# Rounded w_out weights of the feed-forward layers: fetched by GpSimd's casting transfers in place of ScalarE's casts

## The chip, the cores and the metric

The kernel runs on one core of one Trainium2 chip. The metric is the device time of one execution in microseconds (us), the median of the runs. Besides the times there is one execution recorded by the hardware profiler, and its trace.

## The reference

One streaming-encoder block over 512 positions with 1024 features, all in float32, one layer deep, on one sequence:

```python
h = h + 0.5 * _swiglu(_rmsnorm(h, ffn1_norm[i]), ffn1_w_in[i], ffn1_w_out[i])
z = _rmsnorm(h, mix_norm[i]) @ w_in[i]
...
h = h + jnp.concatenate([y_conv, y_gla], axis=-1) @ w_out[i]
h = h + 0.5 * _swiglu(_rmsnorm(h, ffn2_norm[i]), ffn2_w_in[i], ffn2_w_out[i])
gate = jax.nn.sigmoid(_rmsnorm(h, ple_norm[i]) @ ple_w_gate[i])
h = h + gate * (p[i] @ ple_w_proj[i])
```

`_swiglu` multiplies by a first matrix (1024 x 5632: a gate and an up half), takes silu(gate) * up, 2816 features, and multiplies by a second matrix (2816 x 1024), named `ffn1_w_out` or `ffn2_w_out`. The mixer between the two feed-forward layers is a causal convolution beside a chunked gated linear attention; its output matrix is also called `w_out`, but the change does not touch it. Below, w_out is the second matrix of a feed-forward layer.

## The kernel before

**Two parts for each operand.** Every large product is done in float32r, a rounded float32. To keep float32 accuracy each operand is split in a high part, the value rounded to float32r, and a low part, the value minus the high part. A product is then three matmuls that add up in PSUM: high x high, high x low, low x high (`mm3`, L209). For a weight the high part is tile wh and the low part wl; for the activations of the second matrix they are actH and actL; the normalised input of the first matrix appears as hgH and hgL and sums of these.

**How a weight gets there.** `load` (L178) takes a plain float32 tile wr (`raw`, six buffers) and has SP's queue fill it from HBM. `parts` (L205) is `high` then `low`: `high` (L183) takes one of six wh and one of six wl buffers and casts wr into wh on ScalarE; `low` (L193) subtracts wh from wr on VectorE into wl. `added` (L198) is another way to a low part, used for weights of the next stage: ScalarE writes the rounded negative of wr into wl, and a transfer that GpSimd issues adds wr to it. A tile has up to 128 partitions x 1024 numbers, 512 KB.

**A feed-forward layer.** `ffn` (L608) goes over the 22 blocks of 128 hidden features in 11 pairs. Most pairs do the first matrix by Strassen's scheme, in seven units m1 to m7 of 24 matmuls over 256 columns each; in each layer a few pairs at the start are plain (units h0 to h7). The gate products of a pair give tile m, and `act_parts` (L658) splits it into actH (ScalarE) and actL (VectorE). The second matrix is taken in the cuts of L33, four hidden blocks each and a last one of six. `second` (L749) makes for each cut units that it calls pieces: one piece has a weight tile of 4 x 128 rows by 256 columns, and its run does 2 x 4 x 3 matmuls over 512 columns and adds the result to h. The last cut is in two halves of three blocks, so its pieces are 3 x 128 rows (384 KB) and 18 matmuls. Each cut has four pieces, the last one eight: 24 pieces a layer, 48 in all. In the text, piece (4,1) is the one of the last cut for columns 512 to 767 and its second half.

**The order.** The units of a layer stand in one list; pieces of a cut are spread between the units of the pairs that follow (two in each pair, after m2 and after m3), and at the end of the layer those of the last cut follow each other. `drive` (L588) goes over the list; each unit brings jobs with a lead, and a job with lead n is written n units ahead of its unit, those with the larger lead first. A piece has `get` (the plain load, lead 7) and `make` (`parts`, lead `AHEAD` = 4). Class `Ordered` (L36) fixes the order of TensorE's, VectorE's and ScalarE's instructions to the order in which the program writes them; so an instruction that waits holds everything behind it on its engine. For SP's and GpSimd's queues the order is left to the compiler, and so is which buffer of a tag a tile gets. Instructions of the ordered engines show L46 in the profile, the line of that class that calls the engine, whatever line they were written on.

**Work of the next stage.** Hooks at given units, such as ("m4", 10) and ("last", 4) of the first layer, load weights of the mixer and complete their low parts by GpSimd's adding transfers. In these stretches GpSimd has hardly anything else to do.

Of the kernel before, what the change touches and what calls it, by code (L numbers as in the profile page):

```python
# [9 lines left out]
F32R = mybir.dt.float32r  # L10
# [5 lines left out]
P = 128  # L16
# [46 lines left out]
def block_kernel(ctx: ExitStack, tc: tile.TileContext, a: dict, out: bass.AP):  # L63
    nc = tc.nc
    pe, dve, act, pool = (Ordered(tc, e) for e in (nc.tensor, nc.vector, nc.scalar, nc.gpsimd))
# [8 lines left out]
    wp = ctx.enter_context(tc.tile_pool(name="w", bufs=1))  # L74
# [5 lines left out]
    def nm(s):  # L80
        uid[0] += 1
        return f"{s}_{uid[0]}"
# [4 lines left out]
    def bt(dt=F32, s="a"):  # L87
        return big.tile([P, SEQ], dt, tag="A", bufs=NA, name=nm(s))
# [7 lines left out]
    def bank():  # L96
        return pp.tile([P, SEQ], F32, tag="mm", bufs=7, name=nm("ps"))
# [36 lines left out]
    def vec(name, c):  # L134
        return vcols[name, c]
# [42 lines left out]
    def load(src, k0, nk, c0, ncol):  # L178
        r3 = raw(nk, ncol)
        fetch(r3, src, k0, nk, c0, ncol)  # L180
        return r3

    def high(r3):  # L183

        nk, nc_ = r3.shape[1], r3.shape[2]
        hi = wp.tile([P, 1024], F32R, tag="wh", bufs=6, name=nm("wh"))
        lo = wp.tile([P, 1024], F32R, tag="wl", bufs=6, name=nm("wl"))
        h3 = hi[:, :nk * nc_].rearrange("p (k c) -> p k c", k=nk)
        l3 = lo[:, :nk * nc_].rearrange("p (k c) -> p k c", k=nk)
        act.copy(h3, r3)  # L190
        return h3, l3, r3

    def low(w, engine=dve):  # L193
        h3, l3, r3 = w
        engine.tensor_tensor(out=l3, in0=r3, in1=h3.bitcast(F32), op=ALU.subtract)
        return h3, l3
# [8 lines left out]
    def parts(r3):  # L205

        return low(high(r3))

    def mm3(ps, wh, wl, xh, xl, first, last):  # L209
        pe.matmul(ps, wh, xh, start=first, stop=False)  # L210
        pe.matmul(ps, wh, xl, start=False, stop=False)
        pe.matmul(ps, wl, xh, start=False, stop=last)
# [15 lines left out]
    def rows_of(w, k):  # L228

        part, kk = (w[k // 4], k % 4) if isinstance(w, list) else (w, k)  # L230
        return part[0][:, kk, :], part[1][:, kk, :]

    def zblock(w, x, mid={}):

        ps = bank()
        for k in range(DC):
            if k in mid:
                mid[k]()
            wh, wl = rows_of(w, k)
            mm3(ps, wh, wl, *x[k], k == 0, k == DC - 1)  # L240
        return ps
# [344 lines left out]
    AHEAD = 4  # L586
# [21 lines left out]
    def ffn(w_in, w_out, x, gname, given, first, rsb, hooks, plain):  # L608
# [4 lines left out]
        got = {}  # L613
# [135 lines left out]
        def second(cut):  # L749

            f0, f1 = cut
            last = f1 == CUTS[-1][1]
            kn = f1 - f0
            nk = kn // 2 if last else kn
            ps = {}

            def piece(n, g, begin, final, key=None):

                def get():
                    got[f0, n, g] = load(w_out, f0 + g * nk, nk, n * P, 2 * P)  # L760

                def make():
                    got[f0, n, g] = parts(got[f0, n, g])

                def run():
                    left = []
                    wh, wl = got.pop((f0, n, g))
                    for i in range(2):
                        if begin:
                            ps[n + i] = bank()  # L770
                        cs = slice(i * P, (i + 1) * P)
                        for kk in range(nk):
                            k = g * nk + kk
                            f = f0 + k
                            mm3(ps[n + i], wh[:, kk, cs], wl[:, kk, cs], *pairs[f // 2].acts[f % 2],
                                k == 0, k == kn - 1)
                        if final:
                            h = hT[n + i]
                            dve.scalar_tensor_tensor(out=h, in0=ps[n + i], scalar=0.5, in1=h,
                                                     op0=ALU.mult, op1=ALU.add)  # L780
                            if last:
                                hi = bt(F32R, "hgH")
                                act.activation(hi, h, AF.Copy, scale=vec(gname, n + i))
                                left.append((h, hi, vec(gname, n + i)))
                    if key:
                        hooks.get(key, lambda *_: None)()
                    if not left:
                        return []

                    def lower():  # L790
                        for h, hi, g in left:
                            lo = bt(F32R, "hgL")
                            dve.scalar_tensor_tensor(out=lo, in0=h, scalar=g, in1=hi.bitcast(F32),
                                                     op0=ALU.mult, op1=ALU.subtract)
                            nhg.append((hi, lo))

                    lower()
                    for h, *_ in left:
                        norm.add(h)

                return [(7, get), (AHEAD, make)], run

            if not last:
                return [piece(n, 0, True, True, ("g2", f0) if n == 0 else None) for n in range(0, DC, 2)]
            return ([piece(n, 0, True, False, ("last", n)) for n in range(0, 6, 2)],
                    [piece(n, 1, False, True, ("rest", n)) for n in range(0, 6, 2)]
                    + [piece(6, 0, True, False, ("rest", 6)), piece(6, 1, False, True, ("rest", 7))])

# [267 lines left out]
    k0 = zblock(wk[0], hg)  # L1076
# [312 lines left out]
    for k in range(4):  # L1389
        for n in range(3):  # L1390
            w, ps = half[n]
            wh, wl = rows_of(w, k)
# [303 lines left out]
    m1 = [kept(p_, "sq", bufs=3) for p_ in x_]  # L1696
    times(y_, a12, b21, first=True, last=True)
    b2 = [low(later_high(t)) if t is t2[1] else parts(t) for t in t2]
    pool.on, pool.last = True, None
    b3 = [added(later_high(t)) for t in t3]  # L1700
# [13 lines left out]
    body(0, 0, z0, *i0)  # L1714
    body(1, 0, z1, *i1)
    b1 = [parts(t1[0])]
    both = tmp("m", 2 * SEQ, bufs=1).rearrange("p (f c) -> p f c", f=2)
    for i in range(2):
# [76 lines left out]
```

## Time and profile before

| What | us |
|---|---|
| three runs | 947.73, 948.3, 947.78 |
| their median | 947.78 |
| the profiled execution, first to last instruction | 948.1 |
| first feed-forward layer, steady part of the span | 37 to 366 |
| mixer | 366 to 555 |
| second feed-forward layer | 555 to 886 |
| input embedding gate, final norm, output | 886 to 948 |

The bounds of the stages are read from the timeline and rounded to whole microseconds. The profile gives for each engine the busy time, the number of instructions, and the granted TensorE clock. A group of instructions is named by engine, operation and its output and inputs; "128x1024" is partitions by elements. Matmul ends are modelled, so two neighbours may seem to overlap; the distance of their starts is the safer number. The engines are PE (TensorE), PEld (its weight loads), DVE (VectorE), ACT (ScalarE), POOL (GpSimd) and SP (SyncE, which only issues transfers here).

### The profile page before, as it was taken

How to read it: one execution, taken by the hardware profiler on the slowest of the kernel's cores; microseconds unless marked ns; L12 is line 12 of the kernel's file. 1: busy time of each engine (PE TensorE's matmuls, PEld its weight loads, DVE VectorE, ACT ScalarE, POOL GpSimd, SP SyncE). 2: the span in 40 equal slices, each digit the busy share in tenths (PEclk: the TensorE clock that was granted, in tenths of full speed). 3: DMA queues.
4: the chain of work that ended last, by engine and by line, in shares of the span. 5: the costliest groups of instructions: out<-in, count | busy, mean ns of one | idle time of the engine just before them, and what ended most of it. 6: DMA issues, size and time to landing. Idle time of an engine off the chain costs nothing.

```text
span 948.1 us, 14383 instructions
## 1 busy us (share of the span) xinstructions
PE 937.2 (99%) x5768; PEld 833.1 (88%) x5768; DVE 749.2 (79%) x1024; ACT 472.3 (50%) x715; POOL 57.4 (6%) x71
## 2 busy tenths in 40 slices
PE   9999999999999999999999999999999999999996
PEld 7888999999999988888877888999999999998885
DVE  5876888887788566999996749887878787865896
ACT  5752443434433564474564855444434433445882
POOL 0000200000000110101030010000000000000131
PEclk9999999999999999999999999999999999999998
DMA  7532323332333493337453671432243224347463
GB/s 228 170 118 74 95 84 103 121 114 85 104 100 111 133 247 87 89 71 198 112 137 86 156 175 48 132 96 85 89 134 111 68 89 133 96 148 222 92 111 112
DMA packets 107687, 112.89 MB, mean 119 GB/s; under 512 B 5140, under 2 KB 96454, under 8 KB 107621
## 3 DMA queue, kind: packets, MB, share of 16 engines
q1 hardware_dynamic: 101732, 94.67, 32.3%
q0 software_dynamic: 5872, 17.30, 10.2%
q8 instruction: 45, 0.74, 0.3%
q14 instruction: 22, 0.17, 0.1%
q10 hardware_dynamic: 16, 0.00, 0.0%
HBM read 93.61 MB, written 2.10 MB: 101 GB/s over the span
## 4 chain that ended last, share of the span: by engine, by line
PE 98%; DVE 0%; DMA 0%; ACT 0%; POOLq 0%; SPq 0%; issue 0%; DVEq 0%
PE ps L46 97%; PE ax L46 1%; DMA wr<-in_ffn_w_in 0%; DVE y L46 0%; POOLq L1791 0%; ACT ycH L46 0%; DVE yc L46 0%; DVE rs L46 0%; SPq L482 0%; ACT s L46 0%; DVE u L46 0%; DVE wh L46 0%; SPq L447 0%; DVE g L46 0%; DVE s L46 0%
## 5 line engine op out<-in xcount | busy, mean ns | idle before, releaser
L46 PE MATMUL ps<-hgH,wh 128*128 128x256 f32 (+1 forms) x768 | 238.8, 316 | 0.4 <-DVE wh L46 0.4
L46 PE MATMUL ps<-hgH,wl 128*128 128x256 f32 (+1 forms) x768 | 238.1, 315 | 0.0
L46 PE MATMUL ps<-hgL,wh 128*128 128x256 f32 (+1 forms) x768 | 237.6, 314 | 0.0
L46 DVE TENSOR_TENSOR wl<-wr,wh 128x1024 fp32r<-128x1024 f32 (+2 forms) x162 | 189.6, 1181 | 48.0 <-ACT wh L46 47.9
L46 ACT CAST wh<-wr 128x1024 fp32r<-128x1024 f32 (+2 forms) x176 | 176.5, 1019 | 29.4 <-PE ps L46 19.0
L46 PEld LDWEIGHTS ps<-hgH,wh 128*128 128x128 f32 x768 | 146.7, 191 | 10.5 <-ACT hgH L46 1.1
L46 PEld LDWEIGHTS ps<-hgH,wl 128*128 128x128 f32 x768 | 147.0, 191 | 9.1
L46 PEld LDWEIGHTS ps<-hgL,wh 128*128 128x128 f32 x768 | 146.1, 191 | 9.1
L46 PE MATMUL ps<-actH,wh 128*128 128x512 f32 x352 | 137.4, 390 | 0.0
L46 PE MATMUL ps<-actL,wh 128*128 128x512 f32 x352 | 137.3, 390 | 0.0
L46 PE MATMUL ps<-actH,wl 128*128 128x512 f32 x352 | 136.9, 389 | 0.0
L46 ACT ACTIVATE s<-g 128x512 f32<-128x512 f32 x48 | 30.4, 633 | 187.1 <-DVE g L46 187.0
L46 DVE SCALAR_TENSOR_TENSOR cv<-glu,cw,cv 128x502 f32<-128x502 f32 (+24 forms) x120 | 82.1, 739 | 0.6
L46 PEld LDWEIGHTS ps<-actH,wl 128*128 128x128 f32 x352 | 66.1, 188 | 14.0
L46 PEld LDWEIGHTS ps<-actH,wh 128*128 128x128 f32 x352 | 66.2, 188 | 12.8
L46 PEld LDWEIGHTS ps<-actL,wh 128*128 128x128 f32 x352 | 66.2, 188 | 12.6
L46 DVE SCALAR_TENSOR_TENSOR h<-ps,h 128x512 f32<-128x512 f32 x80 | 54.0, 686 | 22.0 <-PE ps L46 21.8
L46 ACT COPY sq<-ps 128x512 f32<-128x512 f32 x38 | 22.1, 585 | 73.8 <-PE ps L46 73.8
L46 DVE TENSOR_TENSOR wl<-sm,wh 128x1024 fp32r<-128x1024 f32 x38 | 46.1, 1221 | 1.2 <-ACT wh L46 0.9
L46 ACT CAST actH<-m 128x512 fp32r<-128x512 f32 x44 | 25.5, 618 | 37.3 <-DVE m L46 37.2
L46 ACT CAST wh<-sm 128x1024 fp32r<-128x1024 f32 x38 | 39.5, 1043 | 5.6 <-DVE sm L46 2.9
L46 DVE TENSOR_TENSOR u<-ps,sq 128x512 f32<-128x512 f32 x17 | 11.7, 691 | 34.8 <-ACT sq L46 34.8
(271 smaller groups left out, 1739.8 us busy)
## 6 DMA issues: line engine op xcount, KB each, us to landing
wr<-in_ffn_w_in SPq DMA_DIRECT2D x84, 512.0 KB
wr<-in_ffn_w_out SPq DMA_DIRECT2D x32, 512.0 KB
wr<-in_w_in SPq DMA_DIRECT2D x20, 512.0 KB
wl<-wr POOLq DMA_DIRECT2D x15, 512.0 KB, 5.2
wr<-in_ffn_w_out SPq DMA_DIRECT2D x16, 384.0 KB
wr<-in_w_out SPq DMA_DIRECT2D x8, 512.0 KB
wq<-in_ple_w_gate SPq DMA_DIRECT2D x8, 512.0 KB
wl<-wq POOLq DMA_DIRECT2D x8, 512.0 KB, 5.1
```

Source lines behind the costliest of these rows:

```text
L46: inst = call(*args, **kwargs)
```

## The change

For the pieces of the second matrix alone, the high part comes from HBM by a transfer of its own. A new function `rounded` takes the wh and wl buffers and has GpSimd issue a transfer whose source is the float32 matrix and whose destination is the float32r tile wh. It is a job of its own, `ask`, with a lead of `AHEAD` + 2 = 6 units. The plain load (`get`) stays with its lead of 7, and `make` (lead 4) is now `low` alone, so ScalarE's cast of these pieces is gone and VectorE's subtraction takes wh from the transfer. The weights of the first matrix, the mixer and the gate are made as before.

```diff
@@ -205,6 +205,13 @@
     def parts(r3):
 
         return low(high(r3))
+
+    def rounded(src, k0, nk, c0, ncol):
+
+        hi, lo = (wp.tile([P, 1024], F32R, tag=t, bufs=6, name=nm(t))[:, :nk * ncol].rearrange(
+            "p (k c) -> p k c", k=nk) for t in ("wh", "wl"))
+        pool.dma_start(out=hi, in_=src[k0 * P:(k0 + nk) * P, c0:c0 + ncol].rearrange("(k p) c -> p k c", p=P))
+        return hi, lo
...
@@ -759,8 +766,11 @@
                 def get():
                     got[f0, n, g] = load(w_out, f0 + g * nk, nk, n * P, 2 * P)
 
+                def ask():
+                    got[f0, n, g, "w"] = rounded(w_out, f0 + g * nk, nk, n * P, 2 * P)
+
                 def make():
-                    got[f0, n, g] = parts(got[f0, n, g])
+                    got[f0, n, g] = low((*got.pop((f0, n, g, "w")), got[f0, n, g]))
...
-                return [(7, get), (AHEAD, make)], run
+                return [(7, get), (AHEAD + 2, ask), (AHEAD, make)], run
```

Each row of such a transfer is 256 numbers of one weight row, 1 KB: 512 rows for a piece of four blocks, 384 for one of three.

## The prediction

> **What bounds the kernel now.** I read the page first, then the busy time by stage, then who waits for whom on TensorE, then the groups and the transfers, and last the timeline of one steady stretch and of the end of each feed-forward layer. The page: busy time, two lines of the 40 slices, and the shares of the chain that ended last.
>
> ```profile
> PE 937.2 (99%) x5768; PEld 833.1 (88%) x5768; DVE 749.2 (79%) x1024; ACT 472.3 (50%) x715; POOL 57.4 (6%) x71
> PEclk9999999999999999999999999999999999999998
> PE 98%; DVE 0%; DMA 0%; ACT 0%; POOLq 0%; SPq 0%; issue 0%; DVEq 0%
> ```
>
> By stage (start, both feed-forward layers, the mixer between them, the tail, and one steady 100 us; the columns are named in the first line), and then all that TensorE's matmuls waited for:
>
> ```profile
> core 0: us, PE busy (x) PEld busy (x) DVE busy (x) ACT busy (x) POOL busy (x), PEclk, DMA share, GB/s
> 37.00:366.00 329.00, 329.00 (x2086) 299.69 (x2085) 257.56 (x312) 152.41 (x211) 12.14 (x14) 1.00 0.40 115
> 366.00:555.00 189.00, 188.76 (x1082) 154.75 (x1081) 159.24 (x265) 104.80 (x195) 25.33 (x28) 1.00 0.49 116
> 555.00:886.00 331.00, 331.00 (x2177) 305.10 (x2177) 257.70 (x303) 152.12 (x201) 5.51 (x7) 1.00 0.39 116
> 886.00:948.00 62.00, 53.56 (x267) 44.75 (x265) 51.66 (x109) 40.70 (x71) 11.61 (x13) 0.95 0.46 102
> 650.00:750.00 100.00, 100.00 (x702) 94.05 (x701) 80.37 (x92) 42.91 (x54) 0.00 (x0) 1.00 0.31 95
> ```
> ```profile
> PE ax L46 <- POOL ident masks.py:199: 1.6, 1, 1.6
> PE ps L46 <- DVE wh L46: 0.4, 1, 0.4
> PE ps L46 <- ACT ycH L46: 0.2, 1, 0.2
> ```
>
> A busy TensorE alone proves little, but here nothing in the two feed-forward stretches (329 and 331 us, the only places that the change touches) waits: TensorE is busy for all of them at the full granted clock, and none of its 2.2 us of waits lies there. The change moves work of ScalarE, which is half idle. So it can win nothing in these stretches; it can only lose, if it makes a weight or an activation late.
>
> **What goes.** 48 casts: 32 pieces of 512 KB and 16 of 384 KB (the last cut).
>
> ```profile
> L46 ACT CAST wh<-wr 128x1024 fp32r<-128x1024 f32 x157 | 161.8, 1045 | 25.6 <-PE ps L46 19.0 <-DMA wr<-in_ffn_w_out 3.3 <-DMA wr<-in_w_in 3.2
> L46 ACT CAST wh<-wr 128x768 fp32r<-128x768 f32 x16 | 13.1, 830 | 2.3 <-issue 1.8 <-ACT wl L46 0.5
> ```
>
> 32 x 1.045 + 16 x 0.830 = 46.7 us of ScalarE's 472.3. Worth on the path: 0, because TensorE waited for ScalarE 0.2 us in all, in the mixer. TensorE's own matmuls cover it.
>
> **What comes, and its traffic.** 48 fetches from POOL. SP's loads of the same weights stay, because VectorE still subtracts the rounded part from the plain one. Queues (packets, MB, share of 16 engines) and issues (KB each, us to landing), then the landing times of all POOL transfers out of wr tiles and of the two into sm tiles:
>
> ```profile
> q1 hardware_dynamic: 101732, 94.67, 32.3%
> q0 software_dynamic: 5872, 17.30, 10.2%
> wl<-wr POOLq DMA_DIRECT2D x15, 512.0 KB, 5.2
> wr<-in_ffn_w_out SPq DMA_DIRECT2D x16, 384.0 KB
> sm<-in_ple_w_gate POOLq DMA_DIRECT2D x2, 512.0 KB, 8.0
> ```
> ```profile
> DMA to landing us min/median/max: 3.3/5.2/9.5
> ```
>
> The new traffic is 32 x 0.524 + 16 x 0.393 = 23.1 MB. At q1's price (32.3/94.67 = 0.34% a MB) that is 7.9% of the span, at q0's (10.2/17.30 = 0.59%, for transfers that also add) 13.6%. On a DMA share of 0.40 neither end binds; I take the lower one, since a cast does not read its destination. SP's loads come a little later beside it. They feed subtractions that end 8.5 us before TensorE's use (below), so 0 on the path.
>
> POOL's issue time is not shown for such a fetch. Its nearest rows (start, us, what) are one add of 128 rows and a pair of 256 rows each:
>
> ```profile
> 433.72 0.86 POOL L46 DMA_DIRECT2D wl<-wr  x1 [3.70 <-ACT wl L46]
> 904.59 2.49 POOL L46 DMA_DIRECT2D sm<-in_ple_w_gate  x2
> ```
>
> 0.86 us for 128 rows and 1.25 for 256 make 0.39 for each further 128: 2.0 us for 512 rows of 1 KB, 1.6 for 384. Bounds: 0.86 if rows cost nothing, 3.4 if all of it goes by rows. I take 2.0 and 1.6: 32 x 2.0 + 16 x 1.6 = 90 us of a POOL that works 17.7 us in both stretches. POOL's other work there is the adds for the next stage's weights; a fetch stands up to 3.4 us ahead of one, and in front of the mixer these have tens of us.
>
> Time L from a free buffer to landing: the nearest row is the fetch from w_gate, 8.0 us for 512 KB, which also adds. Three quarters of the bytes make 6.0, half a microsecond more for shorter rows 6.5. Bounds: below 4.7 (5.2 less the half microsecond for a quarter fewer bytes), above 8.0 x 384/256 = 12.0, if the rows set it. For a 512 KB piece 5.2 to 16.0, I take 8.5.
>
> **The new wait, in the steady stretch.** VectorE's subtraction now waits for this landing instead of for ScalarE. Behind it on VectorE stand the other subtractions, the gate products and the updates of h, which free PSUM. A fetch is asked for six units ahead and its buffer is granted in program order, earliest freed first (my reading of the code; nothing in the trace contradicts it). Counted so, the piece that TensorE begins at 696.59 gets the buffer of a weight whose last matmul starts at 673.73; the first of VectorE's two subtractions at 686.83 is its own.
>
> ```profile
> 673.73 0.28 PE L46 MATMUL ps<-hgH,wl 128*128 128x256 f32 x1
> 696.59 0.40 PE L46 MATMUL ps<-actH,wh 128*128 128x512 f32 x1
> 686.83 2.36 DVE L46 TENSOR_TENSOR wl<-wr,wh 128x1024 fp32r<-128x1024 f32 x2 [0.27 <-ACT wh L46]
> ```
>
> Free at 674.0, wanted by VectorE at 686.8: 12.8 us for an L of 8.5. Nobody waits. Were it later, the subtraction (1.2 us) would still have until 696.6, so about L = 21 us is the point from which TensorE stands still, past the upper bound of 16. Cost 0. Early allocation takes a buffer for about two more units, so some ScalarE casts start when the unit before ends (a Strassen unit is 24 matmuls, and the steady 100 us hold 702, so at most 3.4 us) instead of earlier: 3.4 us out of a lead like the 8.5 us from this subtraction's end at 688.05 to 696.59. Cost 0; without that lead it would be up to 3.4 us a unit.
>
> **The new wait at the end of each layer.** Here cuts of three blocks follow each other and buffers are all taken, so a fetch goes out only as a unit ends. The tightest: piece (4,1) gets its buffer as the matmul that starts at 328.53 ends, 328.8. Behind its subtraction at 334.87 stand the last product m, its cast and its low part actL, which TensorE reads at 340.62; in the second layer the same from 854.2 to 866.06.
>
> ```profile
> 328.53 0.28 PE L46 MATMUL ps<-hgH,wl 128*128 128x256 f32 x1
> 334.87 0.96 DVE L46 TENSOR_TENSOR wl<-wr,wh 128x768 fp32r<-128x768 f32 x1 [1.42 <-ACT wh L46]
> 335.75 0.68 DVE L46 TENSOR_TENSOR m<-u,s 128x512 f32<-128x512 f32 x1
> 336.46 1.14 ACT L46 CAST actH<-m 128x512 fp32r<-128x512 f32 x2 [1.62 <-DVE m L46]
> 337.12 1.29 DVE L46 TENSOR_TENSOR actL<-m,actH 128x512 fp32r<-128x512 f32 x2 [0.69 <-ACT actH L46]
> 340.62 0.39 PE L46 MATMUL ps<-actL,wh 128*128 128x512 f32 x1
> 853.97 0.28 PE L46 MATMUL ps<-hgH,wl 128*128 128x256 f32 x1
> 866.06 0.39 PE L46 MATMUL ps<-actL,wh 128*128 128x512 f32 x1
> ```
>
> From landing to the first half of actL: 0.96 + 0.68 + 1.14/2 + 1.29/2 = 2.9 us. So the fetch may land at 337.7 and 863.2, which is L = 8.9 in both. With L = 6.5 it lands at 335.3, a wait of 0.4 us on VectorE and 0 on TensorE.
>
> **Sum.** 0 for the casts, 0 for the traffic, 0 for either wait: the span stays at 948.1 us. That is 0.3 above the median of the three runs, 947.78, so I predict 947.8. 0.2% is 1.9 us, about what a measurement of this kernel can tell from no change.
>
> **Rivals.** *Late at the ends* (slower): L above 8.9 in the last cuts. For it speak a slowest landing of 9.5 and the upper bound of 12.0; against it the median of 5.2 and that a cast reads no destination. Each us beyond costs one us in each layer: at L = 11, 2 x 2.1 = 4.2, so 952.0; at the bound of 12.0, 954.0.
>
> *POOL's writing of descriptors held up by VectorE* (slower): if each VectorE instruction shut it out, 2.0 us of writing would find only the 19.6 free us in the steady 100: 10.2 us, 1.6 us 8.2, L = 13.1, and 2 x 4.2 = 8.4: 956.2. Against it: the add of 433.72 took only 0.86 us beside this subtraction.
>
> ```profile
> 433.84 1.22 DVE L46 TENSOR_TENSOR wl<-wr,wh 128x1024 fp32r<-128x1024 f32 x1
> ```
>
> The Trainium skill, "SBUF — State Buffer", section "SBUF: two separate sides", warns that a VectorE instruction in a two-port mode keeps GpSimd from writing descriptors, so that its transfers appear to be blocked. The same page ("Who interferes with whom") does not count tensor_tensor, which fills VectorE here, among these; the row above agrees, and no run here shows the other kind.
>
> *A slow cast path* (slower): rows cast at a rate that brings L to 25 us would hold each of 48 pieces for the 4 us beyond 21: 192 us more, 1140. It takes 2.6 times the slowest landing seen.
>
> *Another order of the tail* (either way): the code of the last 62 us leaves the order to the compiler's planner, which may now choose otherwise; TensorE idles 8.4 of these. I give it 2 us: 945.8 or 949.8.
>
> *The transfer does not round* (no change): then the low part is zero; the same instructions run, 947.8.
>
> **Chances.** Hidden 0.52 (own range 947.2 to 948.6), not rounding 0.04: same 0.56. Late ends 0.20, because the point of 8.9 lies inside the bounds of L; held-up writing 0.05, slow cast 0.05, tail to the slow side 0.05: slower 0.35. Tail to the fast side 0.09: faster. The range 945.8 to 954.0 takes in the late ends up to the bound of L and leaves out held-up writing, slow cast and what of the late ends lies past that bound (0.05): 0.15.
>
> **What would show it.** Right: no TensorE wait in 37 to 366 and 555 to 886; 48 casts fewer on ScalarE; fetches of 1 to 3.4 us on POOL that land in 5 to 12; VectorE's waits for ScalarE's wh partly turned into short waits for a transfer. Late ends would show as a TensorE wait for actL near 340 and 866. Wrong: TensorE waiting for wl in the steady stretch, or fewer matmuls than 702 in a steady 100 us.

## The result, and the profile after

The changed kernel takes 955.92 us (median of 4 runs, 953.36 to 956.99) against 947.75 before: a ratio of 1.0077, 95% interval 1.0065 to 1.0088, so 8.2 us more. The forecast was 947.8 with a range from 945.8 to 954.0.

From the page of the changed kernel: busy time, the granted clock in 40 slices, the shares of the chain that ended last, the software queue, then GpSimd's fetches and ScalarE's casts as groups, and the fetches as issues (KB each, median us to landing).

```profile
PE 940.9 (99%) x5768; PEld 835.1 (88%) x5768; DVE 749.4 (79%) x1024; ACT 432.5 (45%) x667; POOL 90.9 (10%) x119
PEclk9999999999999997999999999999999999999998
PE 94%; DMA 2%; DVE 2%; ACT 1%; issue 0%; POOL 0%; POOLq 0%; SPq 0%; ACTq 0%
q0 software_dynamic: 29168, 40.38, 20.1%
L46 POOL DMA_DIRECT2D wh<-in_ffn_w_out x48 | 38.1, 794 | 558.0 <-DVE wl L46 342.7
L46 ACT CAST wh<-wr 128x1024 fp32r<-128x1024 f32 (+1 forms) x128 | 132.0, 1036 | 57.7 <-PE ps L46 52.6
wh<-in_ffn_w_out POOLq DMA_DIRECT2D x32, 512.0 KB, 4.9
wh<-in_ffn_w_out POOLq DMA_DIRECT2D x16, 384.0 KB, 5.6
```

The change did what it says: the casts went from 176 to 128 and 48 fetches came. They are cheaper than forecast. Yet two things are new: the clock has a 7 in the 16th slice (23.9 us each, so about 358 to 382 us), and the chain is TensorE for 94%, not 98%. All that TensorE's matmuls waited for, as in the same view of before:

```profile
PE ps L46 <- ACT hgH L46: 2.9, 1, 2.9
PE ax L46 <- POOL ident masks.py:199: 1.6, 1, 1.6
PE ps L46 <- ACT ycH L46: 0.2, 1, 0.2
```

One wait of 2.9 us, for hgH: not a weight and not an activation of the feed-forward layer, but the mixer's first input. By stretches around it (same columns as in the prediction), the changed kernel first and then the kernel before:

```profile
37.00:361.00 324.00, 324.00 (x2062) 295.30 (x2061) 249.08 (x300) 126.58 (x180) 26.89 (x37) 1.00 0.53 147
361.00:366.00 5.00, 2.09 (x9) 1.16 (x7) 4.81 (x8) 2.85 (x5) 0.00 (x0) 0.89 0.68 160
366.00:376.00 10.00, 10.00 (x29) 7.88 (x29) 4.42 (x11) 1.30 (x3) 1.05 (x1) 0.55 0.08 31
376.00:555.00 179.00, 178.77 (x1028) 146.19 (x1027) 155.74 (x251) 104.85 (x195) 22.27 (x25) 1.00 0.47 116
555.00:886.00 331.00, 331.00 (x2184) 305.31 (x2183) 253.00 (x301) 127.57 (x172) 24.43 (x32) 1.00 0.53 151
```
```profile
361.00:366.00 5.00, 5.00 (x23) 4.13 (x22) 4.70 (x8) 2.38 (x4) 0.00 (x0) 1.00 0.37 105
366.00:376.00 10.00, 10.00 (x53) 8.47 (x52) 3.37 (x10) 2.25 (x3) 1.05 (x1) 1.00 0.20 54
```

Both feed-forward stretches are full, as before. In 361 to 366 TensorE is busy for 2.09 of 5 us, and in the next 10 us it is busy all the time, yet does 29 matmuls in place of 53 at a granted clock of 0.55: its busy time hides a loss. TensorE's order is the same in both kernels, so the start of each matmul can be set against its own start before. That gives the whole account (us, after minus before; matmuls counted from 0):

```
matmul     before    after   later by
27          10.19     8.29      -1.90
2237       363.97   362.39      -1.58   <- last before the wait
2238       364.20   365.70      +1.50   <- first behind it: 3.1 us lost
2263       368.99   375.15      +6.16   <- 4.7 us lost at half the pace
end of span 948.1    954.3      +6.2
```

The 3.1 us and the 4.7 us make 7.7 of the 8.2 (from -1.58 to +6.16). Between matmul 27 and 2237, which is the first layer, and from 2263 to the end, which holds the second layer and the tail, the distance hardly moves. The -1.90 at the start is no gain: the execution profiled before began slowly (see the last section). In all later profiles the time is 1.7 us above the span, so that execution took about 949.8 and not 948.1.

Why hgH was late is read on ScalarE. The timeline of the changed kernel, and below it that of before; "hgH" of the eight blocks of h are the last thing that the mixer waits for, and they stand in ScalarE's order behind the casts wa of w_in.

```profile
326.70 1.14 ACT L46 CAST wa<-wr 128x512 fp32r<-128x512 f32 x2 [6.22 <-DMA wr<-in_w_in]
337.34 1.14 ACT L46 CAST actH<-m 128x512 fp32r<-128x512 f32 x2 [5.61 <-DVE m L46]
343.31 1.14 ACT L46 CAST wa<-wr 128x512 fp32r<-128x512 f32 x2 [4.82 <-DMA wr<-in_w_in]
350.42 0.72 ACT L46 ACTIVATE hgH<-h,vcol 128x512 fp32r<-128x512 f32 x1 [1.89 <-DVE h L46]
364.92 1.34 ACT L46 ACTIVATE hgH<-h,vcol 128x512 fp32r<-128x512 f32 x2 [2.15 <-DVE h L46]
```
```profile
324.66 1.14 ACT L46 CAST wa<-wr 128x512 fp32r<-128x512 f32 x2 [0.74 <-DMA wr<-in_w_in]
338.29 1.14 ACT L46 CAST wa<-wr 128x512 fp32r<-128x512 f32 x2
346.33 1.33 ACT L46 ACTIVATE hgH<-h,vcol 128x512 fp32r<-128x512 f32 x2
362.48 1.34 ACT L46 ACTIVATE hgH<-h,vcol 128x512 fp32r<-128x512 f32 x2 [2.14 <-DVE h L46]
```

The second pair's cast starts 5.0 us later (343.31 against 338.29) because its tile of w_in landed later. The delay reaches hgH by way of VectorE: behind the late casts ScalarE does one more cast, VectorE's subtraction waits for that one, and the update of h, which hgH reads, stands behind this subtraction in VectorE's order. VectorE in the changed kernel:

```profile
348.56 1.23 DVE L46 TENSOR_TENSOR wl<-wr,wh 128x1024 fp32r<-128x1024 f32 x1 [5.48 <-ACT wh L46]
349.70 1.28 DVE L46 SCALAR_TENSOR_TENSOR h<-ps,h 128x512 f32<-128x512 f32 x2
```

The first hgH is 4.1 us later, the last 2.4. TensorE is 1.6 us ahead at that point, and 2.4 + 1.6 = 4.0 us of lateness meet a lead of about one. And the load: SP's issue, and GpSimd's queue before it, first of the changed kernel, then of the kernel before.

```profile
328.69 1.82 POOL L46 DMA_DIRECT2D wa<-wr  x2 [3.78 <-ACT wa L46]
329.93 1.37 POOL L46 DMA_DIRECT2D wh<-in_ffn_w_out  x1
330.75 2.32 POOL L46 DMA_DIRECT2D wa<-wr  x2
331.94 2.77 POOL L46 DMA_DIRECT2D wh<-in_ffn_w_out  x2
334.61 0.37 SPq L176 DMA_DIRECT2D wr<-in_w_in  x1
```
```profile
326.65 1.97 POOL L46 DMA_DIRECT2D wa<-wr  x2 [217.16 <-ACT wa L46]
330.91 1.75 POOL L46 DMA_DIRECT2D wa<-wr  x2 [2.29 <-ACT wa L46]
332.54 1.12 SPq L176 DMA_DIRECT2D wr<-in_w_in  x2
```

SP may issue this load only when the adds wa<-wr have read a plain tile free: 334.61 against 332.54, 2.1 us later. The adds themselves are not slower: the second lands 5.1 us after its issue (329.33 to 334.47), 5.0 before (327.38 to 332.40). They are issued later because the cast of the first pair of w_in blocks starts at 326.70 and not at 324.66: its load takes 6.5 us beside two fetches, 4.8 before. Against TensorE, which is 1.6 to 2 us ahead in this profile, the delay is larger. The best measure is the kernel with the fetches in the second layer alone (below), whose first layer is that of before and whose TensorE keeps within 0.1 us of the changed kernel's up to 338 us. There the first pair's load is issued at 317.86, 2.3 us earlier than the 320.15 of the changed kernel, and the second pair's at 330.68, 3.9 us earlier. The 2.3 us go back to a cast on ScalarE that waited 2.2 us for a matmul of TensorE (316.95; it starts at 314.66 there, without a wait). That fits a cast without a free buffer, which the prediction expected of early allocation.

Then the load does not begin. The packet records show its first packet 1.7 us after the issue in the kernel before, and 4.8 us after the issue in the changed one, at 339.39; there the software queue worked without a gap, from 330.2 to 341.6, through 1776 packets with the 2.2 MB of three fetches and four adds (384 KB and 256 KB each).

### The profile page after: what moved, and what is told of

The parts are those of the page before. It is cut to its first block, busy times and chain, and to the rows that moved or that the text cites. A ratio compares the mean times of both kernels' runs of the same rounds, so it can differ in the third digit from the quotient of the medians.

```text
span 954.3 us, 14382 instructions
## 1 busy us (share of the span) xinstructions
PE 940.9 (99%) x5768; PEld 835.1 (88%) x5768; DVE 749.4 (79%) x1024; ACT 432.5 (45%) x667; POOL 90.9 (10%) x119
## 4 chain that ended last, share of the span: by engine, by line
PE 94%; DMA 2%; DVE 2%; ACT 1%; issue 0%; POOL 0%; POOLq 0%; SPq 0%; ACTq 0%
PE ps L46 92%; PE ax L46 2%; DMA wr<-in_w_in 2%; ACT wa L46 1%; DMA wa<-wr 1%; DVE wl L46 0%; ACT wh L46 0%; DVE h L46 0%; DVE sqacc L46 0%; ACT hgH L46 0%; DVE hgL L46 0%; DVE y L46 0%; ACT sq L46 0%; POOLq L1801 0%; ACT ycH L46 0%
## 5 line engine op out<-in xcount | busy, mean ns | idle before, releaser
L46 ACT CAST wh<-wr 128x1024 fp32r<-128x1024 f32 (+1 forms) x128 | 132.0, 1036 | 57.7 <-PE ps L46 52.6
L46 POOL DMA_DIRECT2D wh<-in_ffn_w_out x48 | 38.1, 794 | 558.0 <-DVE wl L46 342.7
```

Of the source, the lines that this page charges most:

```text
L46: inst = call(*args, **kwargs)
```

## The experiments

Three theories. A: only fetches at the end of the first layer cost anything; they make the loads of w_in late, ScalarE's casts of these hold up hgH, TensorE waits and then runs at half clock. B: VectorE's new wait holds up h and hgL behind it. C: each fetch costs a little.

**Where.** A condition in `piece` chooses the pieces that are fetched; the others keep ScalarE's cast. The diff is against the changed kernel and shows the new lines alone.

```diff
+                by_pool = <condition>
                 def make():
+                    w = got[f0, n, g]
+                    got[f0, n, g] = low((*got.pop((f0, n, g, "w")), w)) if by_pool else parts(w)
...
+                return [(7, get), (AHEAD, make)] + ([(AHEAD + 2, ask)] if by_pool else []), run
```

The condition `gname == "ple_norm"`:

> The fetches in the second feed-forward layer alone; the first layer keeps ScalarE's casts. Theory A (only the fetches of the first layer's last cut cost anything: they make the loads of w_in late, ScalarE's casts of these hold up hgH, TensorE waits 2.9 us and then runs at half clock for some 10 us): no loss, 947.8 within 1 us, and no TensorE wait for hgH. Rival C (each fetch costs a little, spread over both layers): half of the 8.2 us, 951.9.

`not (last and gname == "mix_norm")`:

> The whole change but for the eight pieces of the first layer's last cut, which keep ScalarE's casts. Theory A: 947.8 within 1 us, no TensorE wait near 363. Rival C: 40 of 48 pieces, 947.75 + 8.2 x 40/48 = 954.6.

`last and gname == "mix_norm"`:

> Fetches for the eight pieces of the first layer's last cut alone. Theory A: all of the loss, 953 to 957, with a TensorE wait of 2 to 4 us for hgH near 363 and a granted clock of 0.5 for about 10 us behind it. Rival C: 8 of 48 pieces, 949.1.

Measured: 948.59 (ratio 1.0002, 0.9992 to 1.0012), 948.79 (1.0006, 0.9996 to 1.0015) and 954.76 (1.0070, 1.0049 to 1.0090); the kernel before had 948.11 beside them. The first two show no wait for hgH, the third the 2.9 us again. Forty fetches cost nothing that can be measured, eight cost nearly all of it (0.70% of 0.77%). C is out.

**Which wait.** The kernel before with a transfer that nothing reads; the line with `add_manual_dep` holds each back to the end of a unit, so that it comes at about the time of the real fetch.

```diff
-    NA = 41
+    NA = 40
+    unread = cp.tile([P, 768], F32R, name="unread")
...
+                def ask():
+                    pool.dma_start(out=unread[:, :nk * 256].rearrange("p (k c) -> p k c", k=nk), in_=w_out[...])
+                    tc.add_manual_dep(pool.latest.ins, pe.latest.ins.name, <Sync, DATA>, reason="order")
...
+                return [(7, get), (AHEAD, make)] + ([(AHEAD + 1, ask)] if last and gname == "mix_norm" else []), run
```

> The kernel before, ScalarE's casts and VectorE's waits as they were, but GpSimd also fetches the eight pieces of the first layer's last cut into a tile that nothing reads, each one held back to the end of the unit five ahead (one 2 KB activation buffer fewer, to make room). Theory A (the transfers' traffic and queue delay the loads of w_in): the load that ScalarE waits for near 338 comes some us later, TensorE waits for hgH and the time is 950 to 956. Rival B (VectorE's subtraction waits for the fetch, up to 4.7 us at 335.75 in the changed kernel, and h and hgL stand behind it): that wait is gone here, so 947.8 within 1 us.

Measured: 954.56 (1.0064, 1.0049 to 1.0079), the same wait of 2.9 us for hgH. ScalarE's timeline of this kernel:

```profile
335.93 0.83 ACT L46 CAST wh<-wr 128x768 fp32r<-128x768 f32 x1
343.33 1.14 ACT L46 CAST wa<-wr 128x512 fp32r<-128x512 f32 x2 [6.57 <-DMA wr<-in_w_in]
```

All casts are back on ScalarE and no subtraction waits for a fetch, yet the w_in tile comes at 343.33 and the loss is there. B is not needed for it. In this kernel the adds also stand behind held-back transfers in GpSimd's own order, and the load is late in another way (issued at 336.36, first packet 2.3 us later). So it does not tell queue from traffic, and it does not show that VectorE's waits play no part in the changed kernel.

**HBM or queue.** Again the last cut of the first layer alone, but GpSimd casts out of the plain tile wr.

```diff
-        pool.dma_start(out=hi, in_=src[k0 * P:(k0 + nk) * P, c0:c0 + ncol].rearrange("(k p) c -> p k c", p=P))
+        pool.dma_start(out=hi, in_=src)
...
-                    got[f0, n, g, "w"] = rounded(w_out, f0 + g * nk, nk, n * P, 2 * P)
+                    got[f0, n, g, "w"] = rounded(got[f0, n, g], nk, 2 * P)
```

> As the run with the first layer's last cut alone, but GpSimd's casting transfer takes the weights from the plain tile wr that SP has loaded, not from HBM: the same bytes in the same software queue, and no second reading of HBM. If the backlog of the software queue beside the adds is what holds back the loads of w_in: the loss stays, 952 to 957, and the first packet of the load that is issued near 334 comes again some 3 to 5 us after its issue. If it is the reading of HBM: 947.5 to 949.5.

Measured: 955.39 (1.0065, 1.0048 to 1.0082); load issued at 333.92, first packet at 338.40. No second reading of HBM, the same loss: it is the backlog of GpSimd's transfers and not the reading of HBM. Whether the queue as such holds the load, or the 16 engines that both queues share, is not told apart: from 330.2 to 341.7 the software queue's packets took 1.01 of these engines' time in the changed kernel, 0.91 in this one and 0.47 in the kernel before.

**The adds' share.** The changed kernel, with the first pair of w_in blocks finished by VectorE, so that four adds of 256 KB leave the software queue; and the same edit in the kernel before.

```diff
-    def ahead(src, c0, ncol):
+    def ahead(src, c0, ncol, part=added):
...
-        return [[added(w) for w in high4(load(src, 0, DC, c, P))] for c in range(c0, c0 + ncol, P)]
+        return [[part(w) for w in high4(load(src, 0, DC, c, P))] for c in range(c0, c0 + ncol, P)]
...
-                  ("m4", 10): lambda *_: w_ahead.append(ahead(w_in, D_CONV, 2 * P)),
+                  ("m4", 10): lambda *_: w_ahead.append(ahead(w_in, D_CONV, 2 * P, low)),
```

> The whole change, but the low parts of the first pair of w_in blocks are subtracted by VectorE and not completed by four of GpSimd's adding transfers. If it is the backlog of the one software queue (1.78 MB of adds and fetches without a gap from 330.2 to 341.6) that holds back the next load, it shrinks, the plain tiles come free some 3 us earlier, and the loss goes to half or less: 948 to 952. If the extra traffic of the fetches alone does it, 953 to 957.

> The kernel before with VectorE's subtraction in place of GpSimd's adds for the first pair of w_in blocks, the control for the run that did this to the changed kernel (949.18). If that run took the loss away and gave nothing of its own: 947.5 to 949. If the subtraction is a gain of its own that offsets a loss that is still there: 939 to 943.

(The 1.78 MB in the first of these are a slip: 1776 packets, 2.2 MB.) Measured: 949.18 on the changed kernel (1.0007, 0.9997 to 1.0016) and 947.98 on the kernel before (1.0001, 0.9992 to 1.0011). So the edit gives nothing of its own and takes the loss away: the w_in load starts 1.0 us after its issue, and ScalarE hardly waits for it.

```profile
337.94 1.14 ACT L46 CAST wa<-wr 128x512 fp32r<-128x512 f32 x2 [0.28 <-DMA wr<-in_w_in]
345.33 0.72 ACT L46 ACTIVATE hgH<-h,vcol 128x512 fp32r<-128x512 f32 x1 [0.24 <-DVE h L46]
```

**Three fetches.** The condition `not (last and gname == "mix_norm" and (n, g) in ((4, 1), (6, 0), (6, 1)))`.

> The whole change, but three pieces keep ScalarE's casts: (4,1), (6,0) and (6,1) of the first layer's last cut, whose fetches were issued at 329.93, 331.94 and 333.90 among the adds. If the backlog in the software queue is the cause, these three carry the loss: 947.5 to 950, no TensorE wait for hgH. If the earlier fetches of that cut (314 to 325) already make the w_in loads too late: 952 to 957.

Measured: 949.4 (1.0014, 1.0004 to 1.0023), no wait for hgH. 45 of 48 fetches stay and about 1.3 us of the loss, although the load is still issued late (334.25): the three carry about 7 of the 8 us. The load of w_in in all these kernels, from the packet records (us; first packet of the hardware queue after the issue):

```
kernel                      issued   first packet   delay   median us
before                      332.54      334.27       1.7     947.75
changed                     334.61      339.39       4.8     955.92
last cut alone              334.71      339.42       4.7     954.76
from the plain tile         333.92      338.40       4.5     955.39
nothing reads the fetch     336.36      338.61       2.3     954.56
without the three           334.25      336.52       2.3     949.40
low part by VectorE         332.38      333.42       1.0     949.18
```

Issue and delay together decide: a first packet after 338 goes with the loss, one before 337 without most of it. The Trainium skill, "DMA: Bandwidth & Descriptors", section "Queues, rings and completion order", has each transfer engine take turns between its queues after at most 64 descriptors. By that a load should begin beside a backlog; here it stood for 4.8 us, and nothing that was run shows at which place.

**The casts moved back.** An attempt at a cure, on the changed kernel: the loads of the second pair stay, their casts and adds come later.

```diff
-    w_ahead = []
+    w_ahead, soon = [], []
...
-                  ("last", 4): lambda *_: w_ahead.append(ahead(w_in, 0, 2 * P))})
+                  ("last", 4): lambda *_: (w_ahead.append([]), soon.extend(load(w_in, 0, DC, i * P, P) for i in range(2))),
+                  ("rest", 2): lambda *_: w_ahead[1].append([added(w) for w in high4(soon[0])]),
+                  ("rest", 4): lambda *_: w_ahead[1].append([added(w) for w in high4(soon[1])])})
```

> The whole change, but ScalarE's casts (and GpSimd's adds) of the second pair of w_in blocks are written later: the loads stay at ('last', 4), the work on the first block comes at ('rest', 2) and on the second at ('rest', 4), behind the hgH of the pieces before. Theory A (what costs is that these casts stand in ScalarE's order ahead of hgH and wait for a late load): hgH comes in time, no TensorE wait for it, no half clock, 947 to 950. If the fetches delay hgH in another way, the wait of 2.9 us stays and the time is 953 to 957.

A miss: 957.09 (1.0084, 1.0065 to 1.0103). ScalarE's timeline shows why:

```profile
349.21 1.05 ACT L46 CAST wh<-wr 128x1024 fp32r<-128x1024 f32 x1 [8.50 <-DMA wr<-in_w_in]
352.15 0.72 ACT L46 ACTIVATE hgH<-h,vcol 128x512 fp32r<-128x512 f32 x1 [1.90 <-DVE h L46]
```

The next cast in the order, of the next pair of w_in, waits for its load as well, and h and hgH are behind that one. All loads of w_in are late, so which of their casts stands first does not matter. Theory A holds in its first half and was too narrow in "these casts".

**The clock.** The changed kernel with transposes that nothing reads where TensorE waits.

```diff
-    pb0 = zblock(wb[0], hg)
+    pb0 = zblock(wb[0], hg, {6: lambda: warm_up(26)})
```

> The whole change, with 26 transposes that nothing reads written on TensorE in the place where it waits for hgH (about 3 us at the full clock's 0.11 to 0.12 us each). Theory A with its second half (the wait itself makes the clock fall to one half for some 10 us, which costs 4.7 us more): the wait is filled, the clock stays, the loss is 3 us in place of 8: 950 to 952. If the lower clock comes from something else, 955 to 957.

Measured: 952.77 (1.0040, 1.0025 to 1.0055), 3.2 us below the changed kernel and 0.8 above the range expected. Its stretches, and the longest wait of its matmuls near the end of the first layer:

```profile
361.00:366.00 5.00, 5.00 (x32) 4.37 (x31) 5.00 (x8) 2.86 (x5) 0.00 (x0) 1.00 0.72 169
366.00:376.00 10.00, 9.95 (x54) 8.21 (x53) 5.02 (x12) 2.10 (x4) 1.05 (x1) 1.00 0.23 65
```
```profile
PE ps L46 <- ACT actH L46: 1.2, 1, 1.2
```

With the wait filled, the next 10 us hold 54 matmuls at a clock of 1.00. So the loss has two parts: a late hgH, and the low clock that the idle time brings. The wait for actH comes at 338.7, behind 5.9 us in which VectorE stood idle for a fetch. It is the place that the prediction named for late ends, and about 2 us of what is left of the loss arise there (the distance to the kernel before goes from -1.9 to +0.1 us).

**Asked for later.** The 40 harmless fetches with a lead of four units, against the kernel that has these 40 with six:

```diff
-                return [(7, get), (AHEAD, make)] + ([(AHEAD + 2, ask)] if by_pool else []), run
+                return [(7, get)] + ([(AHEAD, ask)] if by_pool else []) + [(AHEAD, make)], run
```

> The 40 pieces outside the first layer's last cut fetched by GpSimd, but asked for with a lead of four units in place of six, just ahead of the subtraction. The prediction's cover (the landing may be as late as some 21 us in the steady stretch; two units less leave about 14, and a fetch lands in about 5): VectorE waits for the fetch at nearly every piece, TensorE does not: 948 to 949.5. If VectorE's wait holds up the gate products behind it, TensorE waits and the time is 951 or more.

Measured: 958.8 (1.0094, 1.0072 to 1.0116). The steady stretches lose nothing; the second layer's end now does what the first layer's end did, a wait of 4.7 us for hgH near 893 and a low clock behind it. GpSimd's timeline and VectorE's there:

```profile
863.90 0.91 POOL L46 DMA_DIRECT2D wl<-wq  x1 [6.75 <-ACT wl L46]
864.53 1.06 POOL L46 DMA_DIRECT2D wh<-in_ffn_w_out  x1
```
```profile
874.57 0.96 DVE L46 TENSOR_TENSOR wl<-wr,wh 128x768 fp32r<-128x768 f32 x1 [11.22 <-PE ps L46]
875.45 1.28 DVE L46 SCALAR_TENSOR_TENSOR h<-ps,h 128x512 f32<-128x512 f32 x2
```

The last fetch stands in GpSimd's order behind an add that waits for ScalarE, is issued at 864.53 and lands 10 us later, behind that add's packets (neither had a packet before 868.5, while the hardware queue moved its loads); VectorE stands idle for 11.2 us with h behind it. (The row names PE as the releaser, but the fetch's packets end at 874.1, right before the subtraction starts.) Here mechanism B does decide, at another place than the change put it.

**The start.** The kernel before with `warm_up(6)` in place of `warm_up(4)`.

> The kernel before with six transposes that nothing reads in place of four at the start, where its profile shows TensorE waiting 0.43 us for wh at 6.2 us and then a pace of half the clock until 10.2. If a wait of this size already brings the clock down: it is filled, and the first 10 us become 1.5 to 1.9 us shorter: 946 to 946.5 in the executions in which the load is late. If the pace comes from something else: 948.1 to 948.6, for the 0.4 us of transposes.

Measured: 948.11 (ratio 0.9992, 0.9983 to 1.0002), no difference in the median. The 11 executions lie between 947.69 and 948.59, the 15 of the kernel before beside them between 947.71 and 950.04; six of these 15 are at 949.75 or above, none of the 11. The fill may take away the long ones, but the interval does not show it. What the expectation takes for the cause of the slow pace, the wait of 0.43 us, does not fit the other profiles (last section). No kernel here is clearly faster than the one before.

## Why the prediction was wrong

**What bounds it, what goes: right.** Nothing was won, TensorE's matmuls covered the 48 casts.

**The price of a fetch: too high.** Issue 0.79 us in the mean where 2.0 and 1.6 were taken, even below the bound of 0.86; GpSimd's 48 issues are 38 us, not 90. Landing 4.9 us for 512 KB (8.5 taken) and 5.6 for 384 KB (6.5 taken). Traffic 23.1 MB, as worked out; the software queue's share rose by 9.9 points, between the 7.9 and 13.6 of the two prices.

**The new wait in the steady stretch: right.** Cost 0, and even two units less lead cost nothing there. **The new wait at the end of each layer: right for TensorE** as it was put, for actL: VectorE waited 4.7 us for a fetch in the first layer, and actL still came in time. The lead there was about used up: in the kernel with the filled wait, TensorE waited 1.2 us for actH at this place.

**The step that failed** is that a delay of transfers was priced at 0 by a look at the wrong consumers. It stands in three places. On the traffic: "SP's loads come a little later beside it. They feed subtractions that end 8.5 us before TensorE's use (below), so 0 on the path." On POOL's issue time: "a fetch stands up to 3.4 us ahead of one, and in front of the mixer these have tens of us". On early allocation, that some casts start later, "3.4 us out of a lead", at cost 0. But at the end of the first layer SP's loads of w_in feed ScalarE's casts, an add frees the plain tile that the next load needs, and a cast that waits for its load holds up everything behind it on ScalarE, down to hgH of the feed-forward layer's own result. The forecast followed the weights of the layer that is changed through the queues, and not the other transfers in the same queues. In its place the runs showed a load that is issued 2.1 us later (3.9 at equal pace of TensorE) and begins 3.1 us later behind its issue; TensorE then stands for 3.1 us. How the later issue comes about, by a cast that waits for TensorE and a slower first load, is read from the profiles; no run changes either alone.

**What no rival had** is the second part: 3.1 us of idle TensorE cost 7.7 us. "Late ends" had the right sign and one of its two places, at another wait, and priced each us late at one us; with the clock it was 7.7 / 3.1 = 2.5 in this execution. Without the clock's 4.7 us the time would have been 951.2 by this account, inside the range. Held-up writing and a slow cast path fell with the prices above; the tail kept its length (+6.16 at matmul 2263, +6.2 at the end); whether the transfer rounds does not show in a time. And the 948.1 us from which the sum starts are a span, not a time: that execution took about 949.8 us, by its slow start, so that the small difference to the median was luck.

## What to carry to other kernels

When a transfer is moved to another queue, list everything else that is in that queue at that time, and for each what becomes free when it ends: a tile that an add reads is a buffer that a load waits for. In a kernel whose TensorE is full, look first for the place with least lead and ask which in-order engine stands before it; forty of these fetches were free and three carried about 7 of the 8 us. Price a TensorE wait of a few us at more than its length.

## What the hardware showed that was not expected

- A wait of 2.9 us was followed by about 10 us at half the clock (granted 0.55, 29 matmuls in place of 53). In the kernel that casts from the plain tile the profiled execution had a wait of 2.8 us, and then 51 matmuls in the same 10 us; it took 951.73, the other three of that kernel 955.1 to 955.7. So the same wait costs about 4 us more or not. The clock records of the traces tell more. Half the clock lasted 10.24 us in the changed kernel and in the one that asks later, 6.82 with the casts moved back, 3.41 in the last cut alone and with the unread fetch, and nothing from the plain tile: three, two, one and no times 3.41 us, and the full clock before it lasted 105 times 3.41 us in the changed kernel. The Trainium skill, "TensorE: Matmul & The Clock Gate", Part 1, says that the clock is gated by activity in a free-running window of about 3.4 us, so that the effect varies with where the window lies. The traces agree: cut into such windows, TensorE was busy for 0.39 of the last window before the fall in the changed kernel (0.41 or less in the other four with a fall). From the plain tile a window ended in the middle of the wait, at 363.99, the windows on its two sides were busy for 0.55 and 0.54, and the clock stayed. Why the return takes one such window or three is open; the table there in the Trainium skill asks for at least one busy window.
- TensorE goes at half pace from its first matmul in every profile here (0.21 us a transpose, 0.11 later), and the first record of the full clock begins at 10.15 us in the kernel before, at 6.45 in the changed one, and between 4.9 and 11.6 in the others. Where it begins after 8 us, matmul 27 starts at 9.1 to 10.3 us and not at 8.2 to 8.7. That accounts for the -1.90 above, and it may be the 1.9 us between the short and the long executions of one program, of which only one is profiled. The wait of 0.43 us for wh at 6.2 us does not explain it alone: the last cut alone waited 0.7 us there with the full clock from 4.93 us, and went on at full pace.
- A hardware load's first packet came 4.5 to 4.8 us after its issue while the software queue worked through a backlog of casts and adds, against 1.7 us beside adds alone (the kernel before) and 1.0 us beside one fetch (the low part by VectorE).
